# A list scheduler's model of transfers: one shared time replaced by two queues in order, and the program ordered anew under it

## The chip, the core and the metric

One NeuronCore of a Trainium2 chip runs the whole program. The metric is the device time of one execution in microseconds (us), lower is better. "Before" is an already tuned kernel. Five instruction streams run side by side and wait for each other by semaphores: TensorE (PE in the profile), VectorE (DVE), ScalarE (ACT), GpSimd (POOL) and SyncE (SP). SP issues most transfers (DMA queue q1 in the profile), GpSimd some (queue q0).

## The reference, cut to what matters

Two layers, each with two branches computed from one normalised input, then gated, merged and added to the residual. Sequence 512, width 1024, everything in float32.

```python
for l in range(2):
    h = rmsnorm(x, norm_g[l])
    aq, ak, av, az, bqk, bv, bi, bf, bo, bz, ga, gb = split(h @ w_in[l])
    oa = diff_attention(rope(rmsnorm(aq)), rope(rmsnorm(ak)), av, lam)     # 8 heads, two maps each
    ya = (rmsnorm(oa) * silu(az)) @ w_out_a[l]
    mq, mk = split(silu(causal_conv(bqk)))
    hb = mlstm(mq, mk, bv, bi, bf)      # 8 heads: (q k^T * decay matrix) v / max(|row sum|, ...)
    yb = (sigmoid(bo) * rmsnorm(hb) * silu(bz)) @ w_out_b[l]
    u = sigmoid(ga) * ya + sigmoid(gb) * yb
    x = x + u @ w_o[l]
```

## The kernel before, in words

**Pieces.** All weight products are cut into pieces of 512 KB of weights (128 x 1024 floats). A piece is named by its matrix and a number: `qk1`, `bz4`, `wob6`. Each float32 weight is split into a high and a low part so that three matmuls (high x high, high x low, low x high) give nearly float32 precision: SP loads the raw piece into `wr`, ACT casts it to `wh`, DVE subtracts to get `wl`, and PE multiplies. There are two `wr` buffers of this kind, so a load waits until DVE has made the `wl` of the piece two before. Pieces listed in `dlo` take another road (`dload`, L1743): GpSimd transfers `dh`, ACT copies its negative to `dl`, and a second, accumulating transfer of GpSimd makes `dl` the low part; SP and DVE have nothing to do for these. That road is open only from the 17th piece on (`i < 16` returns).

**Seven products.** `bv`, `gb` and `wo` are computed with seven products P1 to P7 in place of eight (as in Strassen's scheme), each of two pieces (`gb.P3` has P3.0 and P3.1). P3, P5, P6 and P7 multiply sums of the activations, called S1 to S4, with a high part `lhS..` and a low part `llS..`; the first digit is the sum (`lhS3`), the next, where it stands, the layer. They are formed once for `bv`, written to DRAM as `dS3h`, `dS3l` and so on, and for `gb` loaded back by SP into `lhS_gb` and `llS_gb` (P7 reads S3). P7, P6, P5 and P4 multiply sums of weight blocks (`wws`, `wwt`), which SP loads and GpSimd completes by accumulating transfers.

**mLSTM heads.** A head's decay matrix is built in the tile `dd`: SP broadcasts rows of DRAM into it with four transfers (512, 384, 256 and 128 columns) and a further one into `em`; DVE adds the mask, ACT takes exponentials, PE computes the scores `ms` and `ms2`, DVE multiplies them onto `dd`, ACT and DVE split `dd` into `sdh` and `sdl`, and PE multiplies with `bv` into `num` and sums the rows into `den`. `dd0_3` is head 3 of layer 0. For the head's norm PE sums squares into `msp_b`; a head listed in `foldM` is folded to half the rows first (one matmul on `fo_b`), a head not listed takes two matmuls (on `msh_b` and `msl_b`). The gate `sbo` (L1153) is ACT's tanh of the product `bo`, read from the PSUM bank that PE fills.

**The order.** No instruction is issued where it is written. Every operation is recorded with its operands (`Recorder.add`) and its nominal cost (`cost`), and `Recorder.schedule` (from L298) then plays the program: whenever an engine is free it takes, among the operations that are ready by the model, the one with the lowest key. The key is the nominal PE time at which the result is needed, plus a bias for each kind of tile (`TUNE["bias"]`) and penalties (`wdiff`, `group`, `drain`, `late`, `risk`; `swpen` for a switch of ACT's function table). Each pick gives the operation an end by the model, and what depends on it becomes ready then. `issue` (L467 to 474) emits the operations in that order; each engine runs its own stream in order. So all instructions have line 474 in the profile, and the loads of ACT's tables line 473. The order in which pieces are multiplied is the list `order` in `TUNE`; the other entries of `TUNE` set when the steps of heads are written relative to it.

For a transfer, the model before has one time `dma`, shared by both queues: the transfer starts when the time and its issuer allow, moves at 150 bytes per ns if it accumulates, 175 from `rows`, 360 from DRAM and 250 else, and the data are taken to have landed a fixed time behind: 

```python
go = s + c if e == "POOL" else s
dma = max(dma, go) + size / self.rate(o)
end[i] = max(dma, go) + (5500.0 if e == "POOL" else 5000.0 if o["a"][1].tensor.name.startswith("rows") else 3000.0)
```

Of the kernel before, what the change touches and what calls it, by code (L numbers as in the profile page):

```python
# [16 lines left out]
DRAM = bass.MemoryType.DRAM  # L17
# [28 lines left out]
    "gls": 2,  # L46
    "glf": 7,
    "attn": (0, 4, 5, 10, 13, 15, 15, 16, 20, 26),
# [3 lines left out]
    "ml": (0, 6, 12, 14, 25, 38),  # L52
    "ahead": 3,
    "lc": 5,
    "slack": 38.3,
    "margin": 0.0,
    "pemargin": 123.8,
    "wait": 278.0,
    "swpen": 141896579.9,
    "smargin": 466.2,  # L60
    "pwait": 0.0,
    "wdiff": 6830.8,
# [4 lines left out]
    "foldM": (0, 1, 2, 3, 4, 5),  # L67
# [5 lines left out]
    "gateA": 1,  # L73
    "gateM": 4,
# [5 lines left out]
    "hfd": 20,  # L80
# [3 lines left out]
    "dlo": ('az0', 'az2', 'az6', 'bo1', 'bo4', 'bo6', 'bo7', 'bqk3', 'bz3', 'ga3', 'gb1', 'gb4', 'qk0.3', 'qk1.2', 'woa4', 'wob1', 'wob5'),  # L84
# [7 lines left out]
    "drain": 62.6,  # L92
    "group": 2214.6,
    "lates": ('bv', 'gb'),
    "risk": 182.7,
    "late": 33.8,
}

# [29 lines left out]
class Recorder:  # L128
# [158 lines left out]
    @staticmethod  # L287
    def rate(o):

        src = o["a"][1]  # L290
        if o["k"].get("accum_op") is not None:
            return 150.0
        return 175.0 if src.tensor.name.startswith("rows") else 250.0 if src.space != DRAM else 360.0
# [4 lines left out]
    def schedule(self):  # L298
# [32 lines left out]
        for i in reversed(range(n)):  # L331
            o = ops[i]
# [5 lines left out]
            key[i] = v - o["cost"]  # L338
        engs = ("PE", "ACT", "DVE", "SP", "POOL")
        ready = {e: [] for e in engs}  # L340
        free = dict.fromkeys(engs, 0.0)
        rt = [0.0] * n
        end = [0.0] * n
        dma = 0.0
        table = 6
        order = []
        at_rows = {"ACT": (0, 0), "DVE": (0, 0)}
        small = False

        def admit(i):  # L350
# [1604 lines left out]
```

## Time and profile before

| | |
|---|---|
| three timed runs | 1321.65, 1321.85, 1322.69 us; median 1321.85 |
| profiled execution | 1324.05 us, of which the span is 1322.3 |
| granted clock of TensorE | 0.999 |
| PE, DVE, ACT, POOL busy | 99%, 81%, 73%, 7% of the span |
| DMA | 192.25 MB, mean 145 GB/s; q1 (SP) 147.02 MB, q0 (GpSimd) 44.05 MB |
| a load of `wr`, issue to landing | 3.6 us median over 172; `dh` 6.4, `dl` 6.7 over 24 each |

How to read it: the span runs from the first to the last instruction of the profiled execution, and its own time is 1.75 us longer. A row of the timeline begins with the start in us from the start of the span and the duration; in brackets behind it stands how long the engine was idle before and what ended that. Matmuls overlap their neighbours, so the step from one start to the next says what a matmul costs PE, not its duration. In a row of a DMA answer the last number is the time from issue to landing.

### The profile page before, as it was taken

The page shows a single profiled execution, that of the slowest core. Times are in us where ns is not written, and L with a number is a line of the kernel's source. Part 1 is how long each engine was busy: PE and PEld are TensorE (multiplying, and loading weights), DVE is VectorE, ACT ScalarE, POOL GpSimd, SP SyncE. Part 2 cuts the span into 40 slices and gives each one's busy share as a digit, 9 for nine tenths or more (in the row PEclk, how much of TensorE's full clock was granted, in tenths as well). Part 3 has the DMA queues.
Part 4 walks back from the last instruction along what each step waited for, and adds up shares of the span by engine and source line. Part 5 has one row for each costly group of instructions (what it writes and reads, how often), then busy time and mean ns, then how long its engine had stood idle before and what let it go on. Part 6 is the DMA issues. An engine that isn't in the chain of part 4 may idle for free.

```text
span 1322.3 us, 18461 instructions
## 1 busy us (share of the span) xinstructions
PE 1310.4 (99%) x6436; PEld 1096.2 (83%) x6436; DVE 1068.1 (81%) x1890; ACT 959.0 (73%) x1940; POOL 88.7 (7%) x112
## 2 busy tenths in 40 slices
PE   9999999999999999999999999999999999999998
PEld 7888888888888788998888888888888887889886
DVE  7898878797668879967888988788965888797686
ACT  5888789896457768863668887888944677697643
POOL 1000000000010100010100100000001101101100
PEclk9999999999999999999999999999999999999999
DMA  5222232226676557776844222321367655588755
GB/s 189 73 80 83 93 100 74 83 65 175 210 207 167 158 139 185 229 212 146 290 136 123 62 81 82 94 88 58 103 172 253 182 154 143 127 204 275 192 139 191
DMA packets 63373, 192.25 MB, mean 145 GB/s; under 512 B 7440, under 2 KB 14224, under 8 KB 63280
## 3 DMA queue, kind: packets, MB, share of 16 engines
q1 hardware_dynamic: 51184, 147.02, 34.6%
q0 software_dynamic: 12096, 44.05, 15.7%
q8 instruction: 51, 0.84, 0.2%
q14 instruction: 42, 0.34, 0.1%
HBM read 178.39 MB, written 12.65 MB: 144 GB/s over the span
## 4 chain that ended last, share of the span: by engine, by line
PE 89%; DMA 4%; ACT 3%; DVE 2%; issue 1%; SPq 0%; DVEq 0%; ACTq 0%
PE qk L474 13%; PE av L474 9%; PE az L474 7%; PE ga L474 7%; PE woa L474 7%; PE bqk L474 7%; PE wob L474 7%; PE wo_P L474 6%; PE bz L474 5%; PE bv_P L474 5%; PE bo L474 5%; PE gb_P L474 3%; PE sc L474 3%; DMA wr<-in_wp_dram 2%; DMA llS_gb<-dS3l 1%; PE ut L474 1%
## 5 line engine op out<-in xcount | busy, mean ns | idle before, releaser
L474 DVE TENSOR_TENSOR wl<-wr,wh 128x1024 fp32r<-128x1024 f32 (+1 forms) x176 | 209.8, 1196 | 46.4 <-ACT wh L474 41.8
L474 ACT CAST wh<-wr 128x1024 fp32r<-128x1024 f32 (+1 forms) x174 | 181.2, 1043 | 71.9 <-DMA wr<-in_wp_dram 25.6
L474 ACT ACTIVATE p<-sc,mx,rq 128x128 f32<-128x128 f32 (+3 forms) x128 | 78.5, 617 | 11.8 <-DVE mx L474 8.5
L474 PE MATMUL qk<-wl,hh 128*128 128x512 f32 x240 | 85.4, 398 | 0.5 <-DVE wl L474 0.5
L474 PE MATMUL qk<-wh,hl 128*128 128x512 f32 x240 | 84.9, 397 | 0.1
L474 PE MATMUL qk<-wh,hh 128*128 128x512 f32 x240 | 84.2, 397 | 0.8 <-ACT hh L474 0.8
L473 ACT ACT_TABLE_LOAD x61 | 78.3, 1283 | 1.1
L474 PE MATMUL woa<-oa,wh 128*128 128x512 f32 x224 | 72.4, 392 | 0.0
L474 PE MATMUL wob<-ob,wh 128*128 128x512 f32 x192 | 59.5, 390 | 0.0
L474 ACT CAST ks<-qkt 64x256 fp32r<-64x256 f32 x128 | 47.1, 368 | 10.9 <-DVE qs L474 8.7
L474 POOL DMA_DIRECT2D dl<-in_wp_dram x24 | 20.9, 872 | 495.4 <-ACT dl L474 466.5
L474 PEld LDWEIGHTS qk<-wh,hh 128*128 128x128 f32 x240 | 45.4, 189 | 9.7 <-ACT hh L474 1.0
L474 PEld LDWEIGHTS qk<-wl,hh 128*128 128x128 f32 x240 | 45.0, 189 | 9.8 <-DVE wl L474 0.9
L474 PEld LDWEIGHTS qk<-wh,hl 128*128 128x128 f32 x240 | 45.2, 189 | 9.4 <-DVE hl L474 0.4
L474 DVE TENSOR_REDUCE mx<-sc 128x2 f32<-128x256 f32 (+1 forms) x64 | 52.3, 817 | 0.7
L474 PEld LDWEIGHTS woa<-oa,wh 128*128 128x128 f32 x224 | 41.7, 188 | 8.4
L474 DVE SCALAR_TENSOR_TENSOR cv<-bqk,par,cv 128x509 f32<-128x509 f32 (+2 forms) x48 | 35.8, 746 | 13.2 <-ACT cv L474 12.3
L474 PE MATMUL az<-hh,wh 128*128 128x512 f32 x112 | 44.7, 399 | 0.0
L474 ACT ACTIVATE sq<-qk 128x64 f32<-128x64 f32 (+1 forms) x144 | 36.5, 266 | 11.0 <-PE qk L474 10.3
L474 PE MATMUL az<-hh,wl 128*128 128x512 f32 x112 | 44.5, 397 | 0.0
L474 PE MATMUL ga<-hh,wh 128*128 128x512 f32 x112 | 44.4, 396 | 0.0
L474 PE MATMUL az<-hl,wh 128*128 128x512 f32 x112 | 44.4, 396 | 0.0
(400 smaller groups left out, 4147.8 us busy)
## 6 DMA issues: line engine op xcount, KB each, us to landing
wr<-in_wp_dram SPq DMA_DIRECT2D x172, 512.0 KB, 3.6
dh<-in_wp_dram POOLq DMA_DIRECT2D x24, 512.0 KB, 6.4
dl<-in_wp_dram POOLq DMA_DIRECT2D x24, 512.0 KB, 6.7
wws_wo<-in_wp_dram POOLq DMA_DIRECT2D x12, 512.0 KB, 7.4
dd<-rows SPq DMA_DIRECT2D x16, 256.0 KB, 4.1
wws_bv<-in_wp_dram POOLq DMA_DIRECT2D x8, 512.0 KB, 6.8
em<-rows SPq DMA_DIRECT2D x16, 256.0 KB, 7.2
wws_gb<-in_wp_dram POOLq DMA_DIRECT2D x8, 512.0 KB, 10.2
```

The lines of the kernel that those rows point to most:

```text
L473: self.tc.keep_in_program_order(self.nc.scalar.preload_act_table_set(self.SET_NAME[o["load"]]))
L474: self.tc.keep_in_program_order(getattr(o["e"], o["fn"])(*o["a"], **o["k"]))
```

## The change

The one shared time becomes two queues, one of SP and one of GpSimd, each in order. While both have work, SP's queue gets 0.45 of the rate and GpSimd's 0.55. Rates are set by kind: 190 bytes per ns for accumulating transfers, 480 for GpSimd's others, 150 from `rows`, 380 for large loads from DRAM, 310 else. Landing comes 1850 ns (SP) or 2300 ns (GpSimd) behind the end.

```diff
         if o["k"].get("accum_op") is not None:
+            return 190.0
+        if o["eng"] == "POOL":
+            return 480.0
+        if src.space == DRAM and src.tensor.name.startswith("rows"):
             return 150.0
-        return 175.0 if src.tensor.name.startswith("rows") else 250.0 if src.space != DRAM else 360.0
+        return 380.0 if src.space == DRAM and math.prod(list(o["a"][0].shape)) >= 131072 else 310.0
+
+    def land(self, o, go, queue):
+
+        z = int(o["eng"] == "POOL")
+        size = 4.0
+        for x in list(o["a"][0].shape):
+            size *= x
+        w = size / self.rate(o)
+        own = 0.55 if z else 0.45
+        t = max(go + (100.0 if z else 350.0), queue[z])
+        r = queue[1 - z] - t
+        if r <= 0:
+            fin = t + w
+        elif w / own <= r / (1.0 - own):
+            d = w / own
+            fin = t + d
+            queue[1 - z] = fin + (r - d * (1.0 - own))
+        else:
+            d = r / (1.0 - own)
+            queue[1 - z] = t + d
+            fin = t + d + (w - d * own)
+        queue[z] = fin
+        return fin + (2300.0 if z else 1850.0)
...
             if o["fn"] == "dma_start":
-                size = 4.0
...
-                go = s + c if e == "POOL" else s
-                dma = max(dma, go) + size / self.rate(o)
-                end[i] = max(dma, go) + (5500.0 if e == "POOL" else 5000.0 if o["a"][1].tensor.name.startswith("rows") else 3000.0)
+                end[i] = self.land(o, s + c if e == "POOL" else s, queue)
```

With it the numbers of `TUNE` are new: some places of `order`, offsets, one piece more in `dlo`, one head less in `foldM`, the penalties, and all of `bias`.

```diff
-        "woa4 woa6 woa0 ga5 woa2 bv.P1 woa5 woa1 bv.P5 bv.P3 bv.P2 bv.P6 bv.P7 bqk0 bo1 bv.P4 bqk6 bo0 bqk1 bz0 bz1 bo4 "
-        "bo2 bz2 bo3 bz4 bz3 bqk2 bqk7 bqk3 bo5 bz5 bo6 bo7 bz6 bz7 gb.P1 gb.P5 gb.P2 gb.P3 gb.P6 gb.P7 wob4 wob6 gb.P4 "
+        "woa6 woa4 ga5 woa2 woa0 bv.P1 woa5 woa1 bv.P5 bv.P3 bv.P2 bv.P6 bqk0 bv.P7 bv.P4 bo1 bqk6 bo0 bz0 bqk1 bz1 bo4 "
+        "bo2 bz2 bo3 bz3 bz4 bqk2 bqk7 bqk3 bo5 bz5 bo6 bo7 bz6 bz7 gb.P1 gb.P5 gb.P2 gb.P3 gb.P6 gb.P7 wob4 wob6 gb.P4 "
...
-    "foldM": (0, 1, 2, 3, 4, 5),
+    "foldM": (0, 1, 3, 4, 5),
...
-    "risk": 182.7,
-    "late": 33.8,
+    "risk": 51441.7,
+    "late": 115.8,
```

What the engines get: PE 6438 matmuls for 6436 (head 2 is no longer folded, one `msp_b` more in each layer); ACT four loads of tables more; `woa6` takes `woa4`'s place on GpSimd's road, and `az2` of layer 0 goes that road too, since `av1` now comes before it.

Three places of the order. The first is SP in layer 0, at the broadcasts for head 3 (`dd0_3`, `em0_3`); `wr78` is the piece `bqk2`, `wr79` is `bqk7` and `wr81` is `bo5`. Before:

```order
L474 DMA em0_2_855<-rows_107 128x512
L474 DMA dd0_3_877<-rows_107 128x512
L474 DMA dd0_3_877<-rows_107 128x384
L474 DMA dd0_3_877<-rows_107 128x256
L474 DMA dd0_3_877<-rows_107 128x128
L474 DMA wr78_905<-in_wp_dram 128x1024
L474 DMA em0_3_878<-rows_107 128x512
L474 DMA wr79_913<-in_wp_dram 128x1024
L474 DMA wr81_925<-in_wp_dram 128x1024
```

After:

```order
L496 DMA wr78_904<-in_wp_dram 128x1024
L496 DMA em0_2_856<-rows_107 128x512
L496 DMA wr79_912<-in_wp_dram 128x1024
L496 DMA dd0_3_876<-rows_107 128x512
L496 DMA dd0_3_876<-rows_107 128x384
L496 DMA dd0_3_876<-rows_107 128x256
L496 DMA dd0_3_876<-rows_107 128x128
L496 DMA em0_3_877<-rows_107 128x512
L496 DMA wr81_924<-in_wp_dram 128x1024
```

The two weight pieces stood behind the four transfers of `dd0_3` and now stand ahead of them.

The second is ACT in layer 0, at the gate `sbo0_7`; `wh92` is `gb.P2.1`, `wh93` and `wh94` are `gb.P3.0` and `gb.P3.1`, `p5_gb0` takes the two halves of P5 out of PSUM and `s1_gb0` those of P1. Before:

```order
L474 ACTIVATE ms_b0_6_1044<-num0_6_1039 128x512
L474 CAST msh_b0_6_1045<-ms_b0_6_1044 128x512
L473 ACT_TABLE_LOAD
L474 ACTIVATE sbo0_7_1008<-bo0_7_991 128x512
L474 CAST wh92_1037<-wr92_1035 128x1024
L474 COPY p5_gb0_1051<-gb0_P5_0_1033 128x512
L474 CAST wh93_1056<-wr93_1054 128x1024
L474 COPY p5_gb0_1051<-gb0_P5_1_1034 128x512
L474 ACTIVATE gb0_0_1062<-s1_gb0_1029 128x2x256
L473 ACT_TABLE_LOAD
L474 ACTIVATE ms_b0_6_1044<-ms_b0_6_1044 128x512 x2
L474 CAST wh94_1060<-wr94_1059 128x1024
```

After:

```order
L496 COPY p5_gb0_1050<-gb0_P5_0_1032 128x512
L496 COPY s1_gb0_1028<-gb0_P1_1_1025 128x512
L496 CAST msh_b0_6_1044<-ms_b0_6_1043 128x512
L495 ACT_TABLE_LOAD
L496 ACTIVATE sbo0_7_1007<-bo0_7_990 128x512
L496 CAST wh92_1036<-wr92_1034 128x1024
L496 CAST wh93_1055<-wr93_1053 128x1024
L496 COPY p5_gb0_1050<-gb0_P5_1_1033 128x512
L495 ACT_TABLE_LOAD
L496 ACTIVATE ms_b0_6_1043<-ms_b0_6_1043 128x512 x2
L495 ACT_TABLE_LOAD
L496 ACTIVATE gb0_0_1061<-s1_gb0_1028 128x2x256
```

Two copies now stand between `ms_b0_6` and its cast, ahead of the gate; `gb0_0` has moved behind `ms_b0_6`'s exponentials, with a load of its own.

The third is SP in layer 1, at the reload of S3 for `gb`'s P7; `wr222` is `wob4` and `wr223` is `wob6`. Before:

```order
L474 DMA lhS21_gb_2149<-dS2h1_1837 128x1024
L474 DMA llS21_gb_2150<-dS2l1_1838 128x1024
L474 DMA wr222_2165<-in_wp_dram 128x1024
L474 DMA lhS31_gb_2155<-dS3h1_1848 128x1024
L474 DMA llS31_gb_2156<-dS3l1_1849 128x1024
L474 DMA wr223_2168<-in_wp_dram 128x1024
```

After:

```order
L496 DMA lhS21_gb_2148<-dS2h1_1836 128x1024
L496 DMA llS21_gb_2149<-dS2l1_1837 128x1024
L496 DMA wr222_2164<-in_wp_dram 128x1024
L496 DMA wr223_2167<-in_wp_dram 128x1024
L496 DMA lhS31_gb_2154<-dS3h1_1850 128x1024
L496 DMA llS31_gb_2155<-dS3l1_1851 128x1024
```

`wob6` has moved ahead of both reloads. In layer 0 that order is as before, but there the reload `lhS20` has moved ahead of the load of `gb.P3.1`.

More of the change, by code (lines that the diff above doesn't have):

```diff
@@ L45 @@
     "gct": 13,
-    "gls": 2,
-    "glf": 7,
-    "attn": (0, 4, 5, 10, 13, 15, 15, 16, 20, 26),
+    "gls": 3,
+    "glf": 4,
+    "attn": (0, 4, 5, 10, 12, 15, 15, 16, 20, 26),
     "a0": 24,
@@ L51 @@
     "a4": 20,
-    "ml": (0, 6, 12, 14, 25, 38),
+    "ml": (0, 6, 12, 12, 25, 36),
     "ahead": 3,
-    "lc": 5,
-    "slack": 38.3,
+    "lc": 4,
+    "slack": 19.8,
     "margin": 0.0,
-    "pemargin": 123.8,
-    "wait": 278.0,
+    "pemargin": 109.4,
+    "wait": 303.6,
     "swpen": 141896579.9,
-    "smargin": 466.2,
+    "smargin": 458.1,
     "pwait": 0.0,
-    "wdiff": 6830.8,
+    "wdiff": 7067.7,
     "wsp": 4,
@@ L72 @@
     "acl": 7,
-    "gateA": 1,
-    "gateM": 4,
+    "gateA": 7,
+    "gateM": 3,
     "actp": (0, 1, 2, 3),
@@ L79 @@
     "slots": 24,
-    "hfd": 20,
+    "hfd": 19,
     "tset": (0, 18),
@@ L83 @@
     "pmask": 0,
-    "dlo": ('az0', 'az2', 'az6', 'bo1', 'bo4', 'bo6', 'bo7', 'bqk3', 'bz3', 'ga3', 'gb1', 'gb4', 'qk0.3', 'qk1.2', 'woa4', 'wob1', 'wob5'),
+    "dlo": ('az0', 'az2', 'az6', 'bo1', 'bo4', 'bo6', 'bo7', 'bqk3', 'bz3', 'ga3', 'gb1', 'gb4', 'qk0.3', 'qk1.2', 'woa4', 'woa6', 'wob1', 'wob5'),
     "dla": 5,
@@ L88 @@
     "qspill": {},
[3 rows of a table removed]
-    "drain": 62.6,
-    "group": 2214.6,
[3 rows of a table added]
+    "drain": 75.4,
+    "group": 1826.8,
     "lates": ('bv', 'gb'),
-    "risk": 182.7,
-    "late": 33.8,
+    "risk": 51441.7,
+    "late": 115.8,
 }
@@ L343, in schedule @@
         end = [0.0] * n
-        dma = 0.0
+        queue = [0.0, 0.0]
         table = 6
@@ L426, in schedule @@
             if o["fn"] == "dma_start":
-                size = 4.0
-                for x in list(o["a"][0].shape):
-                    size *= x
-                go = s + c if e == "POOL" else s
-                dma = max(dma, go) + size / self.rate(o)
-                end[i] = max(dma, go) + (5500.0 if e == "POOL" else 5000.0 if o["a"][1].tensor.name.startswith("rows") else 3000.0)
+                end[i] = self.land(o, s + c if e == "POOL" else s, queue)
             for t in o["tiles"]:
```

10 rows, old and new, of the table TUNE are left out of this document.

## The prediction

> **What bounds the kernel now.** I read the page first, then the waits of TensorE (PE), then the chain of work and the timeline at each place where PE waits. The page's span, its line of engines and the first line of its chain:
>
> ```profile
> span 1322.3 us, 18461 instructions
> PE 1310.4 (99%) x6436; PEld 1096.2 (83%) x6436; DVE 1068.1 (81%) x1890; ACT 959.0 (73%) x1940; POOL 88.7 (7%) x112
> PE 89%; DMA 4%; ACT 3%; DVE 2%; issue 1%; SPq 0%; DVEq 0%; ACTq 0%
> ```
>
> PE is busy for 99% of the span. A new order of the same matmuls can't make them shorter; it can only remove or add gaps between them. The second view bounds the gain, the waits of PE by what ended them (us in total, times, longest):
>
> ```profile
> PE ms L474 <- DVE dd L474: 1.8, 2, 1.0
> PE warm L474 <- DVE ml L474: 1.6, 1, 1.6
> PE qk L474 <- ACT hh L474: 0.8, 1, 0.8
> PE gb_P L474 <- DMA llS_gb<-dS3l: 0.8, 2, 0.5
> PE wo_P L474 <- DVE xr L474: 0.8, 1, 0.8
> PE bv_P L474 <- DVE llS_bv L474: 0.7, 2, 0.3
> PE gb_P L474 <- DMA llS_gb<-dS1l: 0.6, 1, 0.6
> ```
>
> Together 7.1 us, of which 2.4 (warm, qk) is the start of the program, before there is work. So a perfect order of everything behind the start wins about 5 us, and somewhat more with the slower first steps after each wait. Nothing bounds a loss in the same way: each of some 6,400 matmuls has an operand that can come too late.
>
> **The change, part by part.** The new model of transfers costs nothing on the chip; it only decides the order. By the order, PE gets 6438 matmuls for 6436. The profiled execution took 1324.05 us, 1.75 more than its span, and stands 2.2 above the median of the three runs (1321.85). I sum the terms against the 1324.05 and carry the same difference over to the median. Minus is faster.
>
> *Start.* The casts of the first head's input come earlier on ScalarE and VectorE. Of the 2.4 us in the rows above I take back 0.4 (0 to 0.6): **-0.4**.
>
> *The seventh bv product.* PE's timeline in layer 0, start and duration:
>
> ```profile
> 376.34 0.39 PE L474 MATMUL bv_P<-wl,lhS_bv 128*128 128x512 f32 x1
> 376.56 0.39 PE L474 MATMUL bv_P<-wh,llS_bv 128*128 128x512 f32 x1
> 376.92 0.47 PE L474 MATMUL bv_P<-wh,lhS_bv 128*128 128x512 f32 x1
> 377.22 0.40 PE L474 MATMUL bv_P<-wl,lhS_bv 128*128 128x512 f32 x1
> 377.96 0.50 PE L474 MATMUL bv_P<-wh,llS_bv 128*128 128x512 f32 x1 [0.34 <-DVE llS_bv L474]
> 378.30 0.40 PE L474 MATMUL bv_P<-wh,lhS_bv 128*128 128x512 f32 x1
> ```
>
> A step between two 512-column matmuls is 0.22 us (376.34 to 376.56). The next four are 0.36, 0.30, 0.74 and 0.34: 0.86 above 4 x 0.22, of which I lay 0.75 to the late llS and its lhS. Now 12 matmuls of bqk0 (12 x 0.22 = 2.6 us) stand ahead of P7, and 12 more among its first. That is over three times what was missing, so the wait goes in both layers: **-1.5** (-1.5 to -0.7, if bqk0's own input is late). bqk0's weights are then next in line.
>
> *The fourth mLSTM head.* The chain of work at its decay matrix, dd0_3:
>
> ```profile
> 442.33 8.09 DMA wr<-in_wp_dram
> 451.46 1.53 ACT dd L474 x3
> 453.01 1.24 DVE dd L474
> 454.38 0.48 PE ms L474 x2
> ```
>
> The weight piece bqk2 stood on SP behind the four dd transfers and landed after 8.09 us. ScalarE had its cast of that piece ahead of dd's exponentials, so the exponentials, VectorE's product and PE's ms came late: 1.0 of the 1.8 us above, and the rest in layer 1. In the new order bqk2 and bqk7 are issued before the dd transfers, and between the matmul that frees dd's buffer (the last one of num0_1) and ms20_3 stand 46 matmuls, nearly all of 512 columns, of bo3 and bz3 above all: some 10.4 us. They must hold the landing and, behind it, 1.53 + 1.24 for exponentials and product. If dd lands as late as bqk2 did, 8.09 + 2.8 = 10.9 misses by 0.5; if it lands in half of that, nothing is missed. I take the waits as gone, with a slow restart of 0.12 (378.30) each: 1.8 + 0.2 = **-2.0** (-2.4 to +0.6).
>
> *bo7's gate ahead of the fifth gb product.* ScalarE's and then PE's timeline in layer 0:
>
> ```profile
> 546.96 0.62 ACT L474 CAST msh_b<-ms_b 128x512 fp32r<-128x512 f32 x1
> 547.61 1.28 ACT L473 ACT_TABLE_LOAD   x1
> 548.90 0.60 ACT L474 ACTIVATE sbo<-bo 128x512 f32<-128x512 f32 x1
> 550.33 0.59 ACT L474 COPY p_gb<-gb_P 128x512 f32<-128x512 f32 x1
> ```
>
> ```profile
> 548.91 0.28 PE L474 MATMUL gb_P<-lhS_gb,wl 128*128 128x256 f32 x1
> 549.03 0.40 PE L474 MATMUL msp_b<-msh_b,ones 128*128 128x512 f32 x1
> 549.55 0.39 PE L474 MATMUL gb_P<-lhS_gb,wh 128*128 128x256 f32 x1
> ```
>
> The gate sbo0_7 reads bo's PSUM bank, which gb_P takes next: 549.03 to 549.55 is 0.52 for a step of 0.22, 0.3 lost. In the new order two copies come before the cast (p5's, which needs the last matmul of the first half of P5, and one of s1). From that matmul: copies 2 x 0.59, cast 0.62, load 1.28, gate 0.60, 3.7 in all and some 0.2 less by overlap. PE has 20 matmuls of 256 columns at 0.12 (548.91 to 549.03) and two msp_b at 0.22: 2.85. So 0.7 to 0.9 is missed for 0.3, in both layers: **+1.2** (+0.4 to +2.2; the second msp_b, now straight behind the first, may be late too).
>
> *Four more loads of ScalarE's tables.* The group's row:
>
> ```profile
> L473 ACT ACT_TABLE_LOAD x61 | 78.3, 1283 | 1.1
> ```
>
> 4 x 1.283 = 5.1 us more on an engine that is busy for 73%; only two places are near PE. One is above, the other the first third-product matmuls of gb, P3.1, in layer 0. ScalarE before, and the transfers issued there:
>
> ```profile
> 554.64 0.63 ACT L474 ACTIVATE gb<-s_gb 128x512 f32<-128x512 f32 x1
> 555.29 1.28 ACT L473 ACT_TABLE_LOAD   x1
> 556.59 1.30 ACT L474 ACTIVATE ms_b<-ms_b 128x512 f32<-128x512 f32 x2
> 557.79 1.04 ACT L474 CAST wh<-wr 128x1024 fp32r<-128x1024 f32 x1
> ```
>
> ```profile
> wr<-in_wp_dram SPq DMA_DIRECT2D x1, 512.0 KB, 5.9
> lhS_gb<-dS2h SPq DMA_DIRECT2D x1, 512.0 KB, 5.7
> ```
>
> In the new order a second load stands between ms_b and gb0_0: 0.59 + 1.28 + 1.30 + 1.28 + 0.63 + 1.04 = 6.1 to P3.1's cast, against 46 matmuls at 0.12 and four of num (0.8), 6.3. Its weights also go behind lhS20 on SP, where 512 KB took 5.9. Even, by the rows: **+0.4** (0 to +1.2). The Trainium skill (ScalarE: Activation LUTs, What ACT_TABLE_LOAD costs) counts a drain of about 1380 ns with each load, 2.66 us per switch, and advises batching by table set, which speaks against this change. The rows have no such drain: the gate starts at 548.90, when the load that began at 547.61 is over. By the page's figure, as an estimate, the three extra loads near PE would cost 1.38 more each, and the sum would be 4.1 higher; what that would do is the third rival.
>
> *wob6 ahead of P7's operand in layer 1.* SP's issues before, and how long each took to land:
>
> ```profile
> 1212.94 0.32 SPq L474 DMA_DIRECT2D lhS_gb<-dS3h  x1
> 1213.78 0.32 SPq L474 DMA_DIRECT2D llS_gb<-dS3l  x1
> 1214.20 0.39 SPq L474 DMA_DIRECT2D wr<-in_wp_dram  x1
> ```
>
> ```profile
> lhS_gb<-dS3h SPq DMA_DIRECT2D x1, 512.0 KB, 6.5
> llS_gb<-dS3l SPq DMA_DIRECT2D x1, 512.0 KB, 9.2
> wr<-in_wp_dram SPq DMA_DIRECT2D x1, 512.0 KB, 12.6
> ```
>
> They land at 1219.4, 1223.0 and 1226.8, one behind the other, some 3.6 us apart; llS is already 0.5 late. Now wob6 (the wr) goes first. It is released when VectorE has P3.1's low half, before PE's 24 matmuls of P3.1 (24 x 0.12 = 2.9 us); the two operands are released by the last of these 24. So of its 3.6 us some 0.7 remain in front of llS, and all 3.6 if the queue is still behind with wob4. The matmuls that cover llS are about 8.6 us in both orders. **+1.2** (0 to +3.6).
>
> *Head 2's state term unfolded.* Two msp_b matmuls of 512 columns, 2 x 0.22: **+0.5** (no gain: they were not there before).
>
> Sum: -0.4 - 1.5 - 2.0 + 1.2 + 0.4 + 1.2 + 0.5 = **-0.6**. 1324.05 - 0.6 = 1323.45 for an execution like the profiled one, 1321.25 for the median. All other moves (attention, the output products, wo's wait on xr of 0.8, whose matmul keeps its place behind its trigger) I cost at nothing, since PE waits for nothing there in the views; a cover of tenths of a us may be gone among them.
>
> **Rivals.** *The new model is right and the waits go* (faster). Then dd, bv and both llS waits go (1.8 + 0.7 + 0.8 + 0.6, 0.12 for the restart of each of seven, 4.7) with 0.4 of the start, the reloads don't wait, and gate and P3.1 cost 0.4 + 0 with 0.5 for the new matmuls: 5.1 - 0.9 = 4.2, **1317.6**. For it: waits for transfers are what the model was made to see. Against it: P7's operand has the same 8.6 us as before and took 9.2.
>
> *SP's order holds up the reloads* (slower). SP issues in order, so a weight piece ahead of lhS31 and llS31 delays both. It decides if the queue is behind by more than 0.7 us when lhS31 is released: then llS31 costs 3.6, P3.1 behind lhS20 in layer 0 costs 1.2, and the gates 2.2. Sum: -0.4 - 1.5 - 2.0 + 2.2 + 1.2 + 3.6 + 0.5 = +3.6, **1325.4**. For it: the three landings above are one queue at its limit. Against it: wob6 is released 2.9 us ahead.
>
> *The loads of tables reach PE* (slower). If each of the four extra loads lay on PE's path in full, 4 x 1.283 = 5.1 would stand in place of the 1.2 + 0.4 of gates and P3.1: -0.6 - 1.6 + 5.1 = +2.9, **1324.75**. Against it: only three of them are near PE, each with cover. The page on ScalarE speaks for more; the row at 548.90 against it.
>
> *The change does not do what it says*, and the order trades like for like: gains and losses each under a us, **1321.85**, inside the forecast's range.
>
> **How the numbers follow.** Forecast 0.37, trading like for like 0.08, the waits go 0.31, SP's order 0.20, the loads 0.04. What a measurement of this kernel can tell from no change is about 0.2%, 2.6 us. The first passes that, as does 0.05 of the forecast's case, where no new wait comes: faster 0.36. The second and the loads pass it by little, so I leave 0.03 of their 0.24 to no change: slower 0.21. The rest, 0.43, is the same. The forecast's own range is 1319 to 1324.5; with the rivals and the ends of the unknown terms, 1316.0 to 1326.0 leaves out 2 in 10.
>
> **What would show it.** In the profile after: PE's waits no longer list bv_P on llS_bv or ms on dd; they list gb_P on llS from dS3l with over 0.8 and a step of about 1 us ahead of P5's second half, in both layers; loads of tables x65; SP's wr of wob6 lands ahead of llS31. I am wrong if PE's waits behind the start sum to under 2 us or over 8, or if a wait of over 1 us stands at a place that I cost at nothing.

## Result and profile after

The changed kernel takes 1339.24 us (median of 4 runs, 1336.94 to 1340.53) beside 1321.76 for the kernel before (1321.65 to 1322.69): a ratio of 1.0127, 95% interval 1.0112 to 1.0142. It is slower by 1.3%, far outside the range that was forecast. The profiled execution took 1340.53 us.

The page after: span, engines, and the first line of the chain.

```profile
span 1338.7 us, 18518 instructions
PE 1316.8 (98%) x6438; PEld 1095.4 (82%) x6438; DVE 1066.7 (80%) x1887; ACT 963.2 (72%) x1942; POOL 89.7 (7%) x114
PE 82%; DMA 9%; ACT 4%; DVE 3%; issue 1%; SPq 1%; DVEq 0%; ACTq 0%
```

More work is not the reason: DVE's busy time fell by 1.4 us, ACT's rose by 4.2, less than its four more loads of tables (5.1), and PE's rose by 6.4, though it has only two matmuls more. The chain tells where the time went: PE had 89% of it and transfers 4%, now 82% and 9%. Next the waits of PE (us in total, times, longest):

```profile
PE ht L496 <- DVE junk L496: 3.8, 3, 1.9
PE den L496 <- DVE fo_d L496: 2.6, 2, 2.0
PE gb_P L496 <- DMA lhS_gb<-dS3h: 2.4, 1, 2.4
PE warm L496 <- DVE ml L496: 1.6, 1, 1.6
PE num L496 <- DVE ms_b L496: 0.8, 3, 0.5
PE bv_P L496 <- ACT wh L496: 0.8, 2, 0.5
PE bqk L496 <- DVE wl L496: 0.5, 1, 0.5
PE gb_P L496 <- ACT sbo L496: 0.5, 1, 0.5
PE ms L496 <- DVE dd L496: 0.4, 1, 0.4
```

With those not shown, eighteen groups sum to 17.5 us, where nine had 7.8. The longest three had 0.2 in all: ht at the start, den behind fo_d, gb_P on lhS. Two groups upstream say what they have in common, ScalarE's casts of the weight pieces (busy, mean; idle before them; what ended most of it) and VectorE's waits for dd's transfers, a group that the kernel before doesn't have:

```profile
L496 ACT CAST wh<-wr 128x1024 fp32r<-128x1024 f32 x173 | 180.1, 1045 | 104.5 <-DMA wr<-in_wp_dram 43.2
```

```profile
DVE dd L496 <- DMA dd<-rows: 8.9, 7, 2.7
```

Before, the casts stood idle for 71.9 us, 25.6 of them for a landing. So data comes later relative to the order than it did, although the transfers themselves hardly changed: a piece wr took 3.8 us from issue to landing in the median, 3.6 before.

To place the loss I count PE's work up to each matmul (each matmul by the step that its kind usually takes in the kernel before) and compare the two executions at equal work. Work itself grew by 0.45 us. The rest of the loss, after less before, in us:

```
place                                        step
start, to x of layer 0                       +2.3
bv's P2 and bqk0, layer 0 (381)              +1.1
fourth mLSTM head, layer 0 (463)             -1.3
den of the third head, layer 0 (467)         +1.3
heads 4 to 6 and bo7's gate, layer 0         +2.0
wo and the turn to layer 1 (630 to 713)      +3.0
fourth mLSTM head, layer 1 (1123)            -1.5
den of the third head, layer 1 (1126)        +2.8
gb's P7, layer 1 (1237 to 1241)              +3.8
all others, each within 0.7                  +2.4
sum                                         +15.9
```

Three of these places in rows. *Start.* GpSimd's timeline:

```profile
4.64 0.69 POOL L496 DMA_DIRECT2D dh<-in_wp_dram  x1
```

This load is of az2's piece. Its buffer is free, so it goes out 4.6 us into the program, beside the landings on which the first matmuls wait; before, GpSimd issued no transfer in the first 26 us. Its first reader comes at 115 us (times of one ns min/median/max, then first and last start in us):

```profile
L496 ACT ACTIVATE dl<-dh x1: 1062/1062/1062, 115.2 to 115.2; 128x1024 fp32r<-128x1024 f32 x1
```

The chain then has

```profile
2.60 9.31 DMA x<-in_x_dram
11.94 1.15 ACT junk L496 x2
14.20 0.75 DVE junk L496
15.09 0.96 PE ht L496 x4
```

and PE's granted clock behind the gap (stretch; busy PE, PEld, DVE, ACT, POOL; clock; DMA share, GB/s) is

```profile
8.00:16.00 8.00, 4.53 (x20) 2.91 (x21) 5.71 (x9) 5.54 (x10) 0.00 (x0) 0.95 1.01 376
16.00:20.00 4.00, 4.00 (x16) 3.27 (x15) 3.69 (x9) 3.41 (x7) 0.00 (x0) 0.67 0.48 170
```

The kernel before loses as much clock here, somewhat earlier:

```profile
8.00:16.00 8.00, 6.46 (x26) 4.43 (x26) 6.86 (x14) 6.81 (x13) 0.00 (x0) 0.80 0.87 314
```

From 16 to 20 us it has 0.98. So the clock takes 0.05 x 8 + 0.33 x 4 = 1.7 us after, and 0.20 x 8 + 0.02 x 4 = 1.7 before: it is no part of the +2.3.

*den in layer 1*, the chain:

```profile
1116.26 8.54 DMA dd<-rows
1124.90 0.43 DVE dd L496
1125.36 0.70 DVE fo_d L496
1126.10 0.50 PE den L496
```

The plan laid VectorE's mask of the fourth head's dd ahead of fo_d of the third, since dd was to land 5.4 us after its issue. It took 8.5. VectorE works in order, so a late transfer for one head holds up the division of another, and PE with it.

*P7 in layer 1.* SP's issues, PE at the place, and the clock:

```profile
1224.66 0.33 SPq L496 DMA_DIRECT2D wr<-in_wp_dram  x1
1227.49 0.33 SPq L496 DMA_DIRECT2D lhS_gb<-dS3h  x1
1227.87 0.42 SPq L496 DMA_DIRECT2D llS_gb<-dS3l  x1
```

```profile
1234.41 0.28 PE L496 MATMUL num<-sdh,bv 128*128 128x256 f32 x1
1237.08 0.65 PE L496 MATMUL gb_P<-lhS_gb,wh 128*128 128x256 f32 x2 [2.40 <-DMA lhS_gb<-dS3h]
```

```profile
1237.00:1241.00 4.00, 3.86 (x14) 2.98 (x15) 0.69 (x1) 2.34 (x5) 0.00 (x0) 0.57 1.04 389
```

lhS31 lands at 1236.95, 9.45 us after its issue (the plan: 6.7), llS31 at 1240.10, 12.2 after (7.7). PE stands for 2.4 us, then runs at 0.57 of its clock for 4: 0.43 x 4 = 1.7 us more.

### The profile page after: what moved, and what is told of

It is laid out like the page before. It is cut to its first block, busy times and chain, and to the rows that moved or that the text cites. A ratio compares the mean times of both kernels' runs of the same rounds, so it can differ in the third digit from the quotient of the medians.

```text
span 1338.7 us, 18518 instructions
## 1 busy us (share of the span) xinstructions
PE 1316.8 (98%) x6438; PEld 1095.4 (82%) x6438; DVE 1066.7 (80%) x1887; ACT 963.2 (72%) x1942; POOL 89.7 (7%) x114
## 3 DMA queue, kind: packets, MB, share of 16 engines
q1 hardware_dynamic: 51040, 146.50, 34.3%
## 4 chain that ended last, share of the span: by engine, by line
PE 82%; DMA 9%; ACT 4%; DVE 3%; issue 1%; SPq 1%; DVEq 0%; ACTq 0%
PE qk L496 13%; PE av L496 8%; PE az L496 7%; PE ga L496 7%; PE bqk L496 7%; PE wob L496 7%; PE woa L496 6%; PE bz L496 5%; PE bo L496 4%; PE bv_P L496 3%; PE wo_P L496 3%; PE gb_P L496 3%; DMA wr<-in_wp_dram 3%; PE sc L496 3%; DMA dd<-rows 3%; PE num L496 2%
## 5 line engine op out<-in xcount | busy, mean ns | idle before, releaser
L496 ACT CAST wh<-wr 128x1024 fp32r<-128x1024 f32 x173 | 180.1, 1045 | 104.5 <-DMA wr<-in_wp_dram 43.2
L496 PE MATMUL av<-wh,hh 128*128 128x512 f32 x128 | 47.9, 400 | 0.0
L496 PE MATMUL av<-wh,hl 128*128 128x512 f32 x128 | 47.8, 399 | 0.0
L496 PE MATMUL av<-wl,hh 128*128 128x512 f32 x128 | 47.5, 396 | 0.0
L496 ACT CAST uh<-ut 128x128 fp32r<-128x128 f32 (+2 forms) x80 | 29.6, 370 | 21.3 <-PE ut L496 17.5
L496 PE MATMUL bqk<-hh,wl 128*128 128x512 f32 x112 | 44.1, 394 | 0.5 <-DVE wl L496 0.5
L496 PE MATMUL bqk<-hh,wh 128*128 128x512 f32 x112 | 44.1, 394 | 0.3 <-ACT wh L496 0.3
## 6 DMA issues: line engine op xcount, KB each, us to landing
wws_gb<-in_wp_dram POOLq DMA_DIRECT2D x8, 512.0 KB, 10.9
```

Source lines behind the costliest of these rows:

```text
L496: self.tc.keep_in_program_order(getattr(o["e"], o["fn"])(*o["a"], **o["k"]))
```

## The plan and the chip

schedule() gives each instruction a planned start and end, so the last planned end can be set beside the span. I call the difference the *slip*. For each matmul I also took its start in the profile less its planned start, and read this drift at every 10 us of the plan. In every kernel below it grows by 6 to 14 us in small steps; where it grows by more than 0.6 us from one reading to the next I call that a *sudden step*. Steps over 0.6, their number, and what was caught up again (steps below -0.3), all in us:

```
kernel                             plan end   span   slip  sudden steps  caught up
before                               1307.7 1322.3   14.6    7.0 (6)       0
after                                1305.5 1338.7   33.2   23.4 (17)      0
e1 old numbers, new model            1325.8 1357.3   31.5   23.2 (13)      0.7
e2 new numbers, old model            1355.8 1373.7   17.9   13.6 (12)      1.7
e3 landing +2 us, new numbers        1339.8 1348.6    8.8    4.7 (4)       5.0
e5 new model, searched               1302.3 1336.6   34.3   22.6 (14)      0
e6 landing +1 us, searched           1306.2 1338.8   32.6   22.4 (7)       0
e9 landing +2 us, searched           1312.6 1325.2   12.6    8.1 (3)       2.4
e8 old model, searched               1305.3 1317.0   11.7    2.7 (3)       0.4
e10 fitted model, searched           1315.2 1342.8   27.6   16.3 (10)      2.3
e11 fitted +1 us, searched           1319.0 1332.4   13.4    5.2 (3)       2.8
```

The spans are those of the profiled executions. By the median times the slips of e2 and e11 would be 21.8 and 15.7, and no other moves by more than 2.7.

The change bought a plan that is 2.2 us shorter and slips 18.6 more. What the theories have to explain is the slip. *Lost margin*: the old model had transfers land late in its plan, and so left PE room; the new one leaves none. *Bad numbers*: this set of numbers is an unlucky one. *Three places*: single mishaps (the start, dd ahead of fo_d, wob6 ahead of P7's reload), to be mended one by one. PE's own reserve in the plan, the number `pemargin`, is not what makes the difference: it is 123.8 ns in e1 and 109.4 in the change, which slip over 30, and 0 in e8, which slips 11.7.

## Experiments

**e1, the numbers of before under the new model.**

```diff
-    "attn": (0, 4, 5, 10, 12, 15, 15, 16, 20, 26),
+    "attn": (0, 4, 5, 10, 13, 15, 15, 16, 20, 26),
-    "ml": (0, 6, 12, 12, 25, 36),
+    "ml": (0, 6, 12, 14, 25, 38),
...
```

> The kernel after with all numbers of the scheduler (order of pieces, offsets, biases, penalties) as before, so that only the model of transfers is new. Lost margin (the new landing times are right in the median, so about half of the transfers land later than planned, and in-order engines stand behind them): slower than before, 1328 to 1340 us. Bad numbers (the model is harmless, the numbers found under it are not): within 3 us of before, 1319 to 1325. Three places (GpSimd's early load, the mask ahead of fo_d in two heads, wob6 ahead of the reloads): 1322 to 1328, as GpSimd has no load at the start here.

Measured: 1356.39 us (1353.88 to 1359.11), ratio 1.0259 (1.0241 to 1.0278): slower than all three theories had it.

**e2, the change's numbers under the old model.**

```diff
-                end[i] = self.land(o, s + c if e == "POOL" else s, queue)
+                dma = max(dma, go) + size / self.rate(o)
+                end[i] = max(dma, go) + (5500.0 if e == "POOL" else 5000.0 if o["a"][1].tensor.name.startswith("rows") else 3000.0)
...
```

> The kernel before with all numbers of the scheduler from after, so that only the model of transfers is old. Lost margin: the waits for transfers go, 1320 to 1328 us. Bad numbers: still over 1333. Three places: the early load of GpSimd at the start stays (2.3 us), the other places can go, 1324 to 1332.

Measured: 1379.36 us (1375.50 to 1381.30), ratio 1.0429 (1.0409 to 1.0449). Of the ranges given, only "over 1333" of *bad numbers* holds it. Both crossings are slower than both kernels, so the total alone says little. The table does: numbers and model were fitted to each other, and changing one makes the plan longer (1325.8, 1355.8); the slip goes with the model, 33.2 and 31.5 under the new one, 14.6 and 17.9 under the old, whichever numbers are used.

**e3, the change's kernel with every landing planned 2 us later.**

```diff
-        return fin + (2300.0 if z else 1850.0)
+        return fin + (4300.0 if z else 3850.0)
```

> The kernel after with 2000 ns more from a transfer's end to its landing in the model, on both queues, and nothing else. Lost margin: most waits for transfers go, 1320 to 1329 us, and waits of PE in the profile sum to under 12 us for 17. Bad numbers: 1334 or more. Three places: 1326 to 1338, by which of the three places the new order keeps.

Measured: 1351.95 us (1348.54 to 1354.84), ratio 1.0224 (1.0202 to 1.0247). That is far from the 1320 to 1329 of *lost margin* and, by the number, what *bad numbers* had; PE's waits sum to 24.1 us, where under 12 were expected. But the plan itself is 34 us longer for the same matmuls, since the numbers don't suit it, and beyond that plan the slip falls to 8.8.

**e4, the three places mended in the changed kernel.**

```diff
+        self.behind(order, self.find(order, "SP", "wr223_"), self.find(order, "SP", "llS31_gb"))
+        for l in (0, 1):
+            self.behind(order, self.find(order, "DVE", f"dd{l}_3_", "dd", 1), self.find(order, "DVE", f"fo_d{l}_2_"))
+        k = self.find(order, "POOL", "dh19_")
...
+        k = self.find(order, "DVE", "ang_", nth=3)
+        order[k:k] = [lambda: self.nc.vector.memset(dh.bitcast(F32)[:, :1], 0.0), i]
```

> The kernel after with three places of the finished order changed by hand: GpSimd's first load (az2 in layer 0) waits for a one-column memset that VectorE does at about 17 us; VectorE's second mask of head 3 goes behind fo_d of head 2, in both layers; SP's load of wob6 in layer 1 goes behind the two reloads of S3. Three places: 2.3 us at the start, 3 at the masks, 4 at P7, about 1330 us. Lost margin: the same or less at these places (1330 to 1335), since other late transfers remain. Bad numbers: within 3 us of after, since the waits move elsewhere, 1336 to 1340.

Measured: 1336.47 us (1333.05 to 1339.31), ratio 1.0105 (1.0080 to 1.0129): less than 3 us of the 17.5, as *bad numbers* had it (the waits move elsewhere). PE's waits show why:

```profile
PE ms L527 <- DVE dd L527: 2.4, 2, 1.8
PE gb_P L527 <- DMA llS_gb<-dS3l: 2.0, 1, 2.0
```

Den no longer waits, but the fourth head's own ms now does, for the same landing. P7 no longer waits 2.4 us for lhS; it waits 2.0 for llS. SP and PE there:

```profile
1224.29 0.32 SPq L527 DMA_DIRECT2D lhS_gb<-dS3h  x1
1224.71 0.38 SPq L527 DMA_DIRECT2D llS_gb<-dS3l  x1
1225.18 0.42 SPq L527 DMA_DIRECT2D wr<-in_wp_dram  x1
```

```profile
1231.90 0.47 PE L527 MATMUL gb_P<-lhS_gb,wh 128*128 128x256 f32 x2 [0.41 <-DMA lhS_gb<-dS3h]
1235.62 0.39 PE L527 MATMUL gb_P<-llS_gb,wh 128*128 128x256 f32 x1 [1.99 <-DMA llS_gb<-dS3l]
```

Even ahead of wob6, llS31 takes 10.9 us. So the order on SP was not the main thing; GpSimd has issued three 512 KB loads of its own, at 1217.8, 1223.5 and 1225.5.

**e5 to e8, numbers searched anew under four models.** In each, the list of pieces is that of the kernel before, and its priorities were changed at random under one model, a change being kept if the plan's end did not come later. e5 has the new model, e6 and e7 the new one with landings 1 and 2 us later, e8 the old one. The edits, beside the priorities, 190 in each (e5, e6, e7 and e8, in this order):

```diff
-    "pemargin": 123.8,
+    "pemargin": 22.6,
...
-        return fin + (2300.0 if z else 1850.0)
+        return fin + (3300.0 if z else 2850.0)
...
-        return fin + (2300.0 if z else 1850.0)
+        return fin + (4300.0 if z else 3850.0)
...
-    "pemargin": 123.8,
+    "pemargin": 0.0,
...
```

> The new model of transfers as it stands, with another set of numbers: the list of pieces and the allocation are those of the kernel before, and its priorities and penalties were changed at random, 150,000 times, each change kept if the plan's own end did not come later. The plan went from 1325.8 us to an end at 1302.3, 3.2 earlier than the plan of the change (1305.5) and 5.4 earlier than the plan of the kernel before (1307.8). Lost margin: any order fitted to this model runs some 32 us over its plan, as the change's does (33.2) and as the old numbers under it did (31.5), since it lays PE's matmuls right behind landings that come late half of the time: span 1334, time 1336 (1332 to 1340), slower than before although its plan is the shortest of all. Bad numbers, or three places: the slip of the change is that of one unlucky set of numbers; a fresh set slips as before's does (14.6): span 1317, time 1319 (1316 to 1322), faster than before.

Measured: 1336.55 us (1333.96 to 1338.40), ratio 1.0110 (1.0095 to 1.0125). The shortest of all plans slips 34.3. With e1 and the change that is three sets of numbers under this model, and all three slip 31 to 34: *bad numbers* falls.

> As the run with the new model searched again, but each transfer is planned to land 1.0 us later than the new model says, and the numbers were searched under that, for as long and from the same start. The plan ends at 1306.2, where the change's ends at 1305.5. Lost margin: the slip lies between the 32 of no margin and the 9 of 2 us, about 20: span 1326, time 1328 (1324 to 1332), so 8 faster than the same search without the margin, for a plan that is 3.9 longer. Bad numbers, or three places: slip as before's, 14.6: span 1321, time 1323 (1320 to 1326), so 4 slower than the same search without the margin.

Measured: 1339.94 us (1329.48 to 1342.03), ratio 1.0114 (1.0069 to 1.0160). Neither theory as I had put it: 20 was expected of the slip, and it was 32.6. The steps became fewer, 7 for 14, but larger. (One of the four executions took 1329.48, so the slip isn't the same each time.) PE's three longest waits:

```profile
PE gb_P L496 <- DMA llS_gb<-dS3l: 5.8, 2, 3.9
PE qk L496 <- ACT wh L496: 3.5, 2, 2.5
PE wo_P L496 <- ACT wh L496: 3.3, 1, 3.3
```

The plan has P7's llS31 land after 7.8 us here; the chain has it at

```profile
1222.54 11.49 DMA llS_gb<-dS3l
```

3.7 late. One us later for everything thins out the misses, but not these.

> As the two runs beside it, with each transfer planned to land 2.0 us later than the new model says, and the numbers searched under that. The plan ends at 1312.6. Lost margin: the slip is that of the change's numbers under the same margin, 9 (8.8 there), so span 1321.5, time 1323 (1320 to 1327): about the kernel before, some 13 faster than the same search without the margin, though its plan is 10.3 longer. Bad numbers, or three places: slip 14.6: span 1327, time 1329 (1326 to 1332), so 10 slower than the same search without the margin.

Measured: 1326.89 us (1326.56 to 1328.03 for the timed executions), ratio 1.0039 (1.0025 to 1.0053): slip about 12.5, and 9.7 us faster than e5, whose plan is 10.3 shorter. The time lies in the ranges of both theories (1320 to 1327 and 1326 to 1332); what tells them apart is that *lost margin* had e7 13 us faster than e5, and *bad numbers* 10 slower.

> The kernel before with its old model of transfers, and its numbers searched on for as long as the others: the plan ends at 1305.3 for 1307.8. All theories agree here on the slip if the old model's late landings are what protects PE: 14.6 to 18 (the kernel before, and the change's numbers under the old model). Lost margin: span 1320 to 1323, time 1322 to 1325, so nothing or little is won, and it runs over 10 us ahead of the same search under the new model. If instead a longer search by itself wears the margin away, whatever the model, it slips as the change does: span 1337, time over 1335.

Measured: 1319.58 us (1318.81 to 1321.83), ratio 0.9985 (0.9976 to 0.9995). It beats the kernel before by 2 us and the changed one by 20, and is faster than any theory had it. The chain's shares and PE's longest waits:

```profile
PE 96%; DVE 2%; ACT 1%; DMA 0%; issue 0%; SPq 0%; DVEq 0%; ACTq 0%
```

```profile
PE warm L474 <- DVE ml L474: 1.6, 1, 1.6
PE gb_P L474 <- DVE s_gb L474: 1.6, 2, 0.8
```

So a longer search doesn't by itself wear the room away: the same method under the old model gives a plan only 3.0 us longer than e5's and a time 17 us shorter.

**e9, e7's kernel again, for its profile.** (In e7's profiled execution, which took 4643 us, each 512-column matmul took 1.1 us at a granted clock of 1.00, so its steps say nothing of the order.)

> The same kernel as the search under 2.0 us of added landing, run again for a profile of an ordinary execution (the first one's showed each 512-column matmul at 1.1 us). By its time (1326.9 against a plan of 1312.6, with 1.8 around the span) it slips 12.5. Lost margin: what the slip holds beyond the 8 to 11 us that every order of this kernel drifts from its plan in small steps is in sudden steps at waits for late transfers, 22 to 24 us of them with the new model as it stands; here at most 4. If the slip is smaller for another reason (a faster drift), the sudden steps are still over 10.

Measured: 1326.76 us (1324.16 to 1328.36), ratio 1.0031 (1.0018 to 1.0043). Sudden steps 8.1, neither the 4 at most of *lost margin* nor the over 10 of the other theory, and one kind of wait is behind most of them:

```profile
PE ms L496 <- DVE dd L496: 5.5, 4, 2.2
```

Of the waits for llS and for casts of weights, none is over 0.3 us.

**e10 and e11, a model fitted to the traces.** The form of the new model, with rates and latencies that fit the landings of eight traces when the real times of issue are put in; e11 adds 1 us.

```diff
-            return 480.0
+            return 395.0
...
+        a, b = own * both, (1.0 - own) * both
...
-        return fin + (2300.0 if z else 1850.0)
+        return fin + (3320.0 if z else 1490.0)
```

> The new model's form with other numbers in it, fitted to the landings of eight traces when it is given the real times of issue: GpSimd's queue 395 GB/s for 480 and 3.32 us of latency for 2.3, SP's large pieces 322 for 380, both together 0.81 of their rates while they overlap, SP's share of them 0.62. Nothing is added as a margin: the median landing is meant to be right. Given real times of issue, the model of the change has GpSimd's transfers 2.1 to 2.6 us too early in the median, and the fitted one is off by 0 in the median and late by 1.7 at the ninth tenth. The numbers were searched again; the plan ends at 1315.2. If the optimism under joint load is what the change lost by: sudden steps fall from 22 us to some 8, slip 18, span 1333, time 1335. If a model that is right in the median has to slip, whichever numbers it has (only an allowance for the tail protects PE): steps as before, slip 32, span 1347, time 1349.

Measured: 1345.12 us (1342.89 to 1346.40), ratio 1.0166 (1.0147 to 1.0185). Slip 27.6, sudden steps 16.3: so the second theory was nearer. But the premise, a model that is right in the median, holds for SP's transfers alone. The fit, and the 2.1 to 2.6 us that the expectation gives for the change's model, come out of the traces only if GpSimd's accumulating transfers, 60 of its 84, are given the rate of its others; both models have 190 bytes per ns for them. With that rate, and the issue times of e10's own trace, GpSimd's transfers land 1.8 us ahead of e10's model in the median and none over 1 us behind it; SP's land 0.1 ahead, and 21 of 179 over 1 us behind. So room for GpSimd's landings alone doesn't take the slip away. Its waits are again chains in order behind a landing:

```profile
PE den L499 <- DVE fo_d L499: 5.2, 4, 1.6
PE msp_b L499 <- ACT msh_b L499: 5.2, 2, 2.6
PE ms L499 <- DVE dd L499: 3.3, 3, 1.6
```

> As the fitted model beside it with 1.0 us added to each landing, numbers searched again; the plan ends at 1319.0. Optimism under joint load: the ninth tenth is now late by 0.7, so sudden steps of 4 at most, slip 13, span 1332, time 1334, a little ahead of the fitted model without it though its plan is 3.8 longer. If only the worst landings (late by 3 to 5 us) count: slip as with 1 us on the model of the change, where it was 32: span 1351, time 1353.

Measured: 1336.45 us (1334.19 to 1339.41), ratio 1.0103 (1.0084 to 1.0122). Slip 13.4, where 13 had been expected: with 1 us more on both queues the fitted model does what 2 us do on the change's. It doesn't win, for its plan is 13.7 us longer than e8's.

**e12, the start alone.** Of e4's edits only GpSimd's first load:

```diff
+        k = self.find(order, "POOL", "dh19_")
...
+        order[k:k] = [lambda: self.nc.vector.memset(dh.bitcast(F32)[:, :1], 0.0), i]
```

> The changed kernel with one edit: GpSimd's first load of a weight piece (az2's high half), which it issues 4.6 us into the program while the first input, the norm's constants and the first weights still land, waits for VectorE's product on the norm's constants. Nothing else moves. If the load takes the start's landings their share of the engines: the 3.8 us that the run of three edits won in its first 40 us come back in full, 1335.4 (1334 to 1337). If the start's wait has another cause, or the piece is then late for its own cast: 1338 to 1340, no change.

Measured: 1339.25 us (1335.64 to 1339.82), ratio 1.0117 (1.0099 to 1.0135): no change in total. Yet at equal work the start is 3.4 us earlier, about as in e4 (3.8); the second group of PE's matmuls on x (`ht`) comes at

```profile
13.14 0.63 PE ht L519 x4
```

for 15.09, and the clock stays at 1.00 from 8 to 20 us, where the changed kernel lost 1.7 us. Of the 3.4, 2.2 are still there at 607 us, and at 660 nothing is: a weight piece of wo, issued at 642.58, lands after 12.2 us there.

```profile
642.58 12.18 DMA wr<-in_wp_dram
656.07 1.15 DVE wl L519
657.26 4.83 PE wo_P L519 x13
```

So *three places* falls too. A place mended hands its time to the next one where the plan has left no room.

## Why the prediction was wrong

The step that failed is the last of its sum: "All other moves ... I cost at nothing, since PE waits for nothing there in the views". That PE waits for nothing somewhere shows that its operands come in time under the old order; it doesn't show by how much, and a new model of transfers is a change of just that, everywhere at once. Of the 15.9 us, 11.8 stand at moves that the sum had at nothing (GpSimd's load at the start 2.3, den 1.3 and 2.8, wo and the turn to layer 1 3.0, the rest 2.4). Two terms with a price were wrong as well, P7 by 2.6 and the seventh bv product by 2.6, both beyond their upper bounds, at waits for weights and reloads. What the runs show in place of "nothing" is the slip: the plan under the new model leaves no room for late landings, and the execution runs 33.2 us over it, where it ran 14.6 over the old one. The sign by which I wanted to be proved wrong came too: PE's waits behind the start sum to over 8 us, and den waits 2.0 us at a place costed at nothing. Point by point:

- *What bounds the kernel*: right, and so was "nothing bounds a loss in the same way". I then gave that sentence no price.
- *Start*, -0.4: +2.3. The casts did not come earlier: the first one of weights waits for its landing until 9.55 us, before until 8.56. GpSimd's load of az2, which went out at 4.64 us, is one of the moves costed at nothing. Without it, in e12 and e4, the start is 3.4 and 3.8 us earlier; about half of that is the clock, which doesn't drop there and which did drop in the kernel before.
- *Seventh bv product*, -1.5: its wait on llS is gone, as forecast, and bqk0's own weights are the late ones, as its upper bound said; with P2's piece late too it is +1.1 in layer 0, and about nothing in layer 1.
- *Fourth mLSTM head*, -2.0: -1.3 and -1.5 at its place, right, and somewhat more. I did not follow VectorE's order one instruction on: the mask of dd now stands ahead of the third head's fo_d, so den waits, +1.3 and +2.8.
- *bo7's gate*, +1.2: right in kind: gb_P on sbo is in PE's list, with 0.5, in one layer.
- *Table loads*, +0.4 for three more near PE: x65, as forecast, and beside that gate no wait at PE that is put down to one.
- *wob6 ahead of P7's reload*, +1.2, at most 3.6: +3.8. The sign was right, the cause only in part: e4 put wob6 behind, and llS31 still took 10.9 us. The half clock behind the wait, 1.7 us, was in no term.
- *Two msp_b*, +0.5: work grew by 0.45.

None of the rivals had it either. The one on the slower side, *SP's order holds up the reloads*, had its place and not its reach. *The new model is right and the waits go* is the one that the runs contradict most plainly, and the trace of before would have said so. With the real times of issue from that trace put into each model (of SP's 359 transfers 179 have a landing in the trace), measured landing less modelled, in us:

```
model, queue       transfers  median  over 1 us late
old, SP                 179   -1.03         9
old, GpSimd              84   -4.36         0
new, SP                 179    0.00        30
new, GpSimd              84   +0.20        19
```

So the new model is right in the median, and that is what costs: about half of the transfers land later than it says, 49 of the 263 by over 1 us, where the old model had 9. It is not too early for every kind. An accumulating load lands in the new plan no sooner than 6.2 us behind the start of its issue (1.0 for issuing, 0.1, 512 KB at 190 bytes per ns 2.76, and 2.3), and in the changed kernel it takes less in the median:

```profile
dl<-in_wp_dram POOLq DMA_DIRECT2D x25, 512.0 KB, 5.5
```

This count needs no run of the changed kernel; I read the new rates in the diff and did not hold them against the landings.

What the runs show: under the new model three different sets of numbers slip 31 to 34 us, and only a later landing in the plan, by 2 us on this model or 1 us on the fitted one, takes the slip to 9 to 13, where the old model has it (12 to 18). Counted as above in each run's own trace and model, the runs that slip under 18 plan SP's landings 1.0 to 2.0 us and GpSimd's 1.9 to 4.5 us later than they come in the median. e6 has 1.0 and 1.3, e10 0.1 and 1.8, and the three without a margin at most 0.3. That is a pattern over eleven kernels, most models with one search each, and no test of how much each queue needs.

What stays open: why single landings come so late, llS31 of layer 1 above all (3.7 to 6.1 us later than the new model says from the real time of issue, in e4, the changed kernel and e6); `land` fixes a landing when the transfer is issued, so what the other queue issues later is not counted against it, but no run tests whether that is the reason. Also open is why 1 us on the change's model moved the slip so little, and whether the plans of the fitted model are long because of the model or because its numbers were searched for too short a time.

## What to carry to other kernels

A plan that fixes the order of in-order engines needs its transfers late, not right: by the median landing half of them come late, and each of these can stall an engine and all that is queued behind. Before you trust a new cost model, put the issue times of a trace that you have into it and count the landings that it has too early; the median alone, near 0 here on both queues, doesn't show them. And where a search shortens a plan, ask what slack it spent, for PE's waits in the profile before don't show slack.

## What the runs showed of the hardware

After a wait of 1.8 us PE ran for 4 us at 0.57 of its clock (e4, from 1124), after one of 2.4 likewise (the changed kernel, from 1237), and after one of 2.0 at the full 1.00 (the changed kernel, from 1126). So a wait of some 2 us can cost nearly 2 more, and does not always. The two stretches not yet shown, of the changed kernel and of e4:

```profile
1126.00:1130.00 4.00, 3.90 (x16) 2.82 (x17) 2.86 (x5) 3.94 (x6) 0.00 (x0) 1.00 0.09 35
```

```profile
1124.00:1128.00 4.00, 4.00 (x14) 3.29 (x13) 2.83 (x5) 3.95 (x6) 0.00 (x0) 0.57 0.02 4
```

With SP's and GpSimd's queues both loaded, five 512 KB pieces landed in 9.2 us in the changed kernel (1230.89 to 1240.10): 285 GB/s. Two of the five were accumulating loads of GpSimd, for which the new model's shares give 0.45 x 380 + 0.55 x 190 = 276 for the two together. So it was not the sum of the two rates that made llS31 late there.
